# A decoder step on one core: side work held to its place in the order of emission, and the first two row blocks of w_up taken by turns

## The chip, the cores and the metric

The kernel runs on one core of a Trainium2 chip. The metric is the device time of one execution in microseconds (us), the median of several. Five engines share the work: TensorE (PE, matrix products and transposes), VectorE (DVE), ScalarE (ACT), GpSimd (POOL) and SyncE (SP, which only issues transfers). Each engine takes its own instructions strictly in the order in which they stand on it; an instruction that waits holds up all that stand behind it.

## What is computed

One layer of a hybrid decoder, for a prompt of 2048 tokens and 32 sample tokens (8 sequences of 4), with a model width of 1024, all in float32:

```
h = rms_norm(x, norm_pre_mix)
q, k, v, z1, z2, g_a, g_b = project_inputs(h, w_in, b_gate)
...
    outs.append(o)                       # three groups of dilated windows
    lses.append(lse)
o_a = merge_dilations(outs, lses)        # softmax over the groups' log sums
...
merged = g_a * (o_a @ w_ao) + g_b * (o_b @ w_bo)
x = x + rms_norm(merged @ w_out, norm_post_mix)
h2 = rms_norm(x, norm_pre_ffn)
f = jnp.square(jax.nn.relu(h2 @ w_up)) @ w_down
x = x + rms_norm(f, norm_post_ffn)
```

The branch `o_b` is a chunked gMLP gate. The sample tokens attend to caches of 128, 512 and 2048 old rows beside their own.

## The kernel before

**Products.** Each float32 matrix is split into a high and a low part, and a product is three matmuls (high by high, high by low, low by high). The high part is a cast on ACT, the low part a subtraction on POOL or DVE (L264 and L268 for the weights of the first stages, L1303 and L1304 in the feed-forward part, L311 and L312 for transposed rows). PE is fed from these.

**Stages.** The prompt is taken in two halves (s = 0, with the sample tokens, and s = 1). For each half come the projections and the attention for six pairs of a head pair and a window group (`project`, `attention`), the gMLP gate, the mix and the output rows (`out_rows`, with the norms). Then `ffn` does w_up for half 0, w_down for half 0, and the same for half 1. In the profile: attention of half 0 from 95 to 285 us and, as its tail, on to about 395; gMLP and mix of half 0 to 737, output rows to 880; attention of half 1 to 1190; gMLP and mix to 1515, output rows to 1600; w_up and w_down behind that. The feed-forward products are Strassen's seven products of half-size blocks (`SEVEN`): `up` takes 16 row blocks u of w_up, for each the seven products p in order, and gathers each product into the blocks that use it.

**The main chain in attention.** PE makes the scores (L670), DVE adds the mask and takes the minimum (L672, listed as ISA or CUSTOM_DVE), ACT takes the exponential (L676), PE transposes and multiplies by the values (L718), and ACT or DVE copies the result out (L175, L177).

**Side work.** What has no place of its own in this is written as Python generators in four lanes. Lane 0 has the attention itself, the norms and other steps of the main line. Lane 1 has `merge` (the softmax over the window groups, 16 blocks in each half, fetched from DRAM into `junk`; lines L778 to L795), `moved` (normed rows of the output to the channel layout `h2`, each half) and `differences` (differences of the blocks of `h2`, by `differ`, L1271 to L1274). Lane 2 has `sample_attention` (L880, L881, L917, L926 on DVE and L927, L929 on POOL), `pre_mix_behind` (the norm of the next half's prompt rows: L357, L359, L361 on ACT, L363 on DVE) and the sample's gate. Lane 3 has `weight_sums`, which adds blocks of w_up and w_down in DRAM by accumulating transfers that POOL issues (L1253), for use in Strassen's products. `tick()`, called between the matmuls of the main line, takes one step of lanes 0, 1 and 2; lane 3 is stepped each time that a set number of columns has gone through PE. `drain` takes all steps that a lane still has.

**The order on an engine.** The order in which the Python code emits instructions is not the order in which they stand on an engine. A scheduler lays all instructions on its own simulated timeline and places each where its operands are ready by that timeline; so an instruction that the timeline holds for ready early can move up past instructions that were emitted before it, main or side. `tc.issue_after(ins)` around an emission forbids that: what is emitted inside stands on its engine behind `ins`. It makes no wait, only an order; L1247 uses it in the kernel before.

Of the kernel before, what the change touches and what calls it, by code (L numbers as in the profile page):

```python
# [2 lines left out]

# [1 line left out]

# [7 lines left out]
AF = mybir.ActivationFunctionType  # L13
# [48 lines left out]
DIFFS = ("t1", "v", "t3", "t4")  # L62
FORMS = ("b11", "b21", "b22") + DIFFS
HALF_T = (TMAX // 2, HALF // 2)


def shape_constants():
# [27 lines left out]
def hybrid_step(ctx: ExitStack, tc: tile.TileContext, ins: dict, outs: list):  # L95
    nc = tc.nc
# [89 lines left out]
    def push(lane, gen):  # L186
        lanes[lane].append(gen)
        return gen

    def step(lane):  # L190
        while lanes[lane]:
            try:
                next(lanes[lane][0])
                return True
            except StopIteration:
                lanes[lane].popleft()
        return False

    def tick(some=(0, 1, 2)):
        for lane in some:  # L200
            step(lane)
# [555 lines left out]
    def merge(s, hp):  # L757

        mt = sm.tile([P, D], F32, tag="t", bufs=1, name="junk")

        def fetch(b):
            m3 = mt[:, (b % 2) * 3 * UW : (b % 2 + 1) * 3 * UW].rearrange("p (g c) -> p g c", g=3)
            nc.sync.dma_start(m3, us[s][hp][b * P : (b + 1) * P])
            return m3

        m3_next = fetch(0)
        for _ in range(6):
            yield
        for b4 in range(2):
            o4 = sm.tile([P, 512], F32, tag="o4", bufs=1, name="o4")  # L770
            for j in range(4):
                b = b4 * 4 + j
                m3 = m3_next
                if b < 7:
                    m3_next = fetch(b + 1)
                nm, l = m3[:, :, 128:130], m3[:, :, 130:132]
                lo = sm.tile([P, 2], F32, tag="mg0", name="lo")
                nc.vector.tensor_reduce(lo, nm.rearrange("p g h -> p h g"), AX, ALU.min)  # L778
                e3 = sm.tile([P, 3, 2], F32, tag="mg1", name="e3")
                nc.vector.tensor_tensor(e3, nm, lo.unsqueeze(1).to_broadcast([P, 3, 2]), ALU.subtract)  # L780
                nc.scalar.activation(e3, e3, AF.Exp, scale=-1.0)
                el = sm.tile([P, 3, 2], F32, tag="mg2", name="el")
                nc.vector.tensor_tensor(el, e3, l, ALU.mult)
                den = sm.tile([P, 2], F32, tag="mg3", name="den")
                nc.vector.tensor_reduce(den, el.rearrange("p g h -> p h g"), AX, ALU.add)
                rd = sm.tile([P, 2], F32, tag="mg4", name="rd")
                nc.vector.reciprocal(rd, den)
                nc.vector.tensor_tensor(e3, e3, rd.unsqueeze(1).to_broadcast([P, 3, 2]), ALU.mult)
                U = m3[:, :, :P].rearrange("p g (h d) -> p g h d", h=2)
                nc.vector.tensor_tensor(U, U, e3.unsqueeze(3).to_broadcast([P, 3, 2, 64]), ALU.mult)  # L790
                yield
                o1 = o4[:, j * P : (j + 1) * P]
                nc.gpsimd.tensor_tensor(o1, m3[:, 0, :P], m3[:, 1, :P], ALU.add)
                nc.gpsimd.tensor_tensor(o1, o1, m3[:, 2, :P], ALU.add)
                yield  # L795
            for _ in range(6):
                yield
            pt = ps.tile([P, 512], F32, tag="t", name="pt")
            for j in range(4):
                nc.tensor.transpose(pt[:, j * P : (j + 1) * P], o4[:, j * P : (j + 1) * P], ident)  # L800
            cs = slice(b4 * 512, b4 * 512 + 512)
            split(oa[:, hp, 0, cs], oa[:, hp, 1, cs], pt, nc.vector)
            yield
# [319 lines left out]
    def out_rows(s, behind=None):  # L1123
# [50 lines left out]
        def moved():  # L1174

            for b in range(n_rows):
                y, n = of(b)
                if s == 1:
                    y = sm.tile([P, D], F32, tag="x", name="xt")
                    nc.sync.dma_start(y, n1_d[b * P : (b + 1) * P])  # L1180
                    for _ in range(4):
                        yield
                for _ in range(3):
                    if paces[0] < 4 * (b + 1) + 2:
                        yield
                while paces[0] < 4 * (b + 1):
                    yield
                for _ in to_h2(s, y, n, b * P):
                    yield
                    yield  # L1190
# [65 lines left out]
    def differences(s):  # L1256

        n = HALF_T[s]
        for k in range(4):
            u, l = (sm.tile([P, 2, TMAX // 2], F32, tag="x", name="xt")[:, :, :n] for _ in range(2))  # L1260
            nc.sync.dma_start(u, h2_d[s][k])
            nc.sync.dma_start(l, h2_d[s][k + 4])
            for _ in range(4):
                yield
            for i, out in enumerate(differ(u[:, 0, :], u[:, 1, :], l[:, 0, :], l[:, 1, :], u[:, 0, :], l[:, 1, :], l[:, 0, :])):
                nc.sync.dma_start(hd_d[s][i, k], out)
            yield
# [50 lines left out]
    def ffn():  # L1318
# [56 lines left out]
        def product_bank(s):  # L1375
            if s == 0:
                return po[0].tile([P, 1024], F32, tag="d", name="pd")
            return po[0].tile([P, 512], F32, tag="e", name="pe", bufs=6)
# [25 lines left out]
        def up(s, ops):  # L1404
            n = HALF_T[s]
            at = {X11: 0, X21: 1, X22: 2, X12: 5}
            ws = weight_stream([up_form(a, u) for u in range(16) for a, _, _ in SEVEN])
            for u in range(16):
                o = u % 2 * 7 * n
                blk = [ov[:, o + i * n : o + (i + 1) * n] for i in range(7)]  # L1410
                X = {x: blk[i] for x, i in at.items()}
                for p, (a, b, uses) in enumerate(SEVEN):
                    w = next(ws)
                    x = ops[b]
                    pt = product_bank(s)
                    for k in range(4):
                        mults(s, pt, w[:, :, k], x[k], k == 0, k == 3)
                        if k in (1, 3):
                            tick()
                    gather(result(s, pt), uses, X)  # L1420
                    for q in ((), (), (), (X22,), (X11,), (X21,), (X12,))[p]:
                        nc.scalar.activation(X[q], X[q], AF.Relu, scale=1.0 if q in (X11, X12) else -1.0)
                        nc.scalar.square(X[q], X[q])
                    if p == 5:
                        nc.sync.dma_start(f_d[s][u, :, 0:3], ov[:, o : o + 3 * n].rearrange("p (i c) -> p i c", i=3))
                differ(X[X11], X[X12], X[X21], X[X22], blk[3], blk[4], blk[6])
                nc.sync.dma_start(f_d[s][u, :, 3:7], ov[:, o + 3 * n : o + 7 * n].rearrange("p (i c) -> p i c", i=4))

        def f_form(s, form, g):
            return f_d[s][4 * g : 4 * g + 4, :, FORMS.index(form)].rearrange("u p c -> p u c")  # L1430
# [303 lines left out]
```

## Time and profile before

| | |
|---|---|
| median of 3 runs | 2915.31 us (2912.81 to 2915.8) |
| the profiled execution | 2921.58 us, span of the profile 2919.9 us |
| PE busy | 2846.7 us, 97% of the span |
| DVE, ACT, POOL busy | 1274.9, 1247.7, 1258.7 us, 44, 43 and 43% |
| granted clock of PE, mean | 0.99 |

The span is the time from the first to the last instruction that the profile shows. "Busy" leaves out waiting. The granted clock is the share of full speed at which PE was let run in a stretch: 1.00 is the upper of its two levels (2.4 GHz), 0.50 the lower (1.2 GHz), and what lies between is a mean over a stretch that has both. A releaser, behind "<-", is the instruction or transfer that came last before a waiting instruction could start.

### The profile page before, as it was taken

How to read it: one execution, taken by the hardware profiler on the slowest of the kernel's cores; microseconds unless marked ns; L12 is line 12 of the kernel's file. 1: busy time of each engine (PE TensorE's matmuls, PEld its weight loads, DVE VectorE, ACT ScalarE, POOL GpSimd, SP SyncE). 2: the span in 40 equal slices, each digit the busy share in tenths (PEclk: the TensorE clock that was granted, in tenths of full speed). 3: DMA queues.
4: the chain of work that ended last, by engine and by line, in shares of the span. 5: the costliest groups of instructions: out<-in, count | busy, mean ns of one | idle time of the engine just before them, and what ended most of it. 6: DMA issues, size and time to landing. Idle time of an engine off the chain costs nothing. (4 is left out here: it accounts for less than half of the span.)

```text
span 2919.9 us, 45510 instructions
## 1 busy us (share of the span) xinstructions
PE 2846.7 (97%) x17434; PEld 2586.2 (89%) x17434; DVE 1274.9 (44%) x2208; ACT 1247.7 (43%) x2439; POOL 1258.7 (43%) x1098
## 2 busy tenths in 40 slices
PE   8998999989999999999999999999999999999998
PEld 8997999989888888888888999999999888878887
DVE  4558356452363344430024555443343644452235
ACT  5443452213453444431135544454343654454334
POOL 3346333453213344243341344445555744445553
PEclk9999999999999999999999999999999999999999
DMA  5755545553658444444326877576665765676655
GB/s 165 195 167 159 151 117 154 146 156 94 189 172 235 126 120 124 109 110 106 81 94 220 282 252 254 181 250 207 204 200 189 238 208 183 197 264 203 192 187 173
DMA packets 463691, 515.00 MB, mean 176 GB/s; under 512 B 25457, under 2 KB 359857, under 8 KB 454258
## 3 DMA queue, kind: packets, MB, share of 16 engines
q1 hardware_dynamic: 452384, 475.06, 51.0%
q0 software_dynamic: 10944, 36.97, 7.0%
q8 instruction: 137, 2.24, 0.3%
q14 instruction: 80, 0.66, 0.1%
q10 hardware_dynamic: 146, 0.07, 0.0%
HBM read 396.44 MB, written 182.68 MB: 198 GB/s over the span
## 5 line engine op out<-in xcount | busy, mean ns | idle before, releaser
L284 PE MATMUL pg<-act,wh 128*128 128x352 f32 (+3 forms) x3424 | 945.5, 354 | 2.8 <-DVE xt L1095 2.0
L1304 POOL TENSOR_TENSOR wf<-raw,wf 128x512 fp32r<-128x512 f32 x444 | 627.5, 1415 | 703.1 <-ACT wf L1303 652.9
L284 PEld LDWEIGHTS pg<-act,wh 128*128 128x128 f32 x3424 | 613.8, 191 | 52.5 <-DVE xt L1095 2.3
L284 PE MATMUL pg<-act,wl 128*128 128x352 f32 (+3 forms) x1712 | 604.2, 353 | 3.3 <-POOL wl L268 3.3
L1303 ACT CAST wf<-raw 128x512 fp32r<-128x512 f32 x444 | 274.9, 620 | 496.4 <-PE pd L1393 188.4
L268 POOL TENSOR_TENSOR wl<-raw,wh 128x512 fp32r<-128x512 f32 (+1 forms) x212 | 273.8, 1318 | 345.9 <-ACT wh L264 319.8
L1393 PE MATMUL pd<-act,wf 128*128 128x264 f32 x2880 | 366.7, 287 | 10.7 <-ACT act L1303 4.9
L1393 PEld LDWEIGHTS pd<-act,wf 128*128 128x128 f32 x2880 | 358.5, 191 | 11.9 <-ACT act L1303 5.1
L284 PEld LDWEIGHTS pg<-act,wl 128*128 128x128 f32 x1712 | 325.3, 190 | 30.4 <-POOL wl L268 3.6
L1493 PE MATMUL pe<-wf,act 128*128 128x512 f32 (+1 forms) x984 | 224.3, 389 | 0.3 <-POOL wf L1304 0.2
L1493 PEld LDWEIGHTS pe<-wf,act 128*128 128x128 f32 x984 | 181.6, 188 | 42.1 <-POOL wf L1304 0.6
L264 ACT CAST wh<-raw 128x1024 fp32r<-128x1024 f32 (+1 forms) x105 | 106.5, 1015 | 259.3 <-PE pg L284 202.8
L1402 DVE TENSOR_TENSOR ov<-pd,ov 128x528 f32<-128x528 f32 x140 | 96.3, 704 | 203.5 <-PE pd L1393 202.9
L1393 PE MATMUL pd<-pair,wf 128*128 128x264 f32 x1440 | 183.9, 284 | 0.3 <-POOL wf L1304 0.3
L1393 PE MATMUL pe<-act,wf 128*128 128x512 f32 x768 | 182.6, 392 | 0.1
L1393 PEld LDWEIGHTS pd<-pair,wf 128*128 128x128 f32 x1440 | 178.2, 188 | 0.5 <-POOL wf L1304 0.5
L1393 PEld LDWEIGHTS pe<-act,wf 128*128 128x128 f32 x768 | 143.8, 188 | 32.9 <-issue 0.3
L1304 DVE TENSOR_TENSOR act<-flat,act 128x1024 fp32r<-128x1024 f32 (+1 forms) x76 | 101.8, 1342 | 157.5 <-ACT act L1303 157.2
L1402 DVE TENSOR_TENSOR ov<-pe,ov 128x512 f32<-128x512 f32 x136 | 91.5, 687 | 136.8 <-PE pe L1393 125.9
L676 ACT ACTIVATE ov<-ov 128x256 f32<-128x256 f32 (+1 forms) x192 | 91.7, 478 | 123.9 <-DVE ov L672 121.3
L1393 PE MATMUL pd<-oa,wf 128*128 128x264 f32 x1056 | 135.3, 284 | 0.0
L1393 PEld LDWEIGHTS pd<-oa,wf 128*128 128x128 f32 x1056 | 131.0, 188 | 0.1
(301 smaller groups left out, 4205.3 us busy)
## 6 DMA issues: line engine op xcount, KB each, us to landing
raw<-in_w_in_dram SPq DMA_DIRECT2D x84, 512.0 KB, 4.4
raw<-up_sums SPq DMA_DIRECT2D x128, 256.0 KB, 4.4
raw<-down_sums SPq DMA_DIRECT2D x128, 256.0 KB, 3.9
flat<-f SPq DMA_DIRECT2D x48, 528.0 KB, 4.4
raw<-in_w_up_dram SPq DMA_DIRECT2D x96, 256.0 KB, 3.2
raw<-in_w_down_dram SPq DMA_DIRECT2D x96, 256.0 KB, 3.9
flat<-f SPq DMA_DIRECT2D x48, 512.0 KB, 3.8
f<-ov SPq DMA_DIRECT2D x16, 1056.0 KB
```

The lines of the kernel that those rows point to most:

```text
L264: nc.scalar.copy(wh[:, :o], raw[:, :o])
L268: eng.tensor_tensor(wl[:, c], raw[:, c], wh[:, c].bitcast(F32), ALU.subtract)
L284: nc.tensor.matmul(pt[:, :n], a[:, o : o + P], b, start=(i == 0 and j == 0), stop=(i == last and j == 2))
L676: nc.scalar.activation(pb[:, h, :w], pb[:, h, :w], AF.Exp, scale=-1.0, bias=stats[:, u, h : h + 1], accum_out=stats[:, u, 2 + h : 3 + h],)
L1303: nc.scalar.copy(high, raw)
L1304: eng.tensor_tensor(low, raw, high.bitcast(F32), ALU.subtract)
L1393: nc.tensor.matmul(pt[:, o : o + n], w[:, a], x[:, b, c : c + n], start=first and j == 0, stop=last and j == 2)
L1402: nc.vector.tensor_tensor(X[to], res, X[add], ALU.add)
L1493: nc.tensor.matmul(pts[i][:, cs], x[k][:, c, t * P : (t + 1) * P], w[:, d, 0, cs], start=k == 0 and j == 0, stop=k == 15 and j == 2,)
```

## The change

Each step of lanes 1 and 2 is now wrapped so that what it emits stands, on PE, DVE, ACT and POOL, behind the last instruction that was emitted on that engine before the step. For lane 3 the same holds on POOL alone. Lane 0 stays free. In `merge` a block has one more empty step (three in place of two), and in `moved` (half 1) and `differences` eight steps in place of four lie between the fetch of a block and its use. In `up` for half 0 the first 14 products, those of row blocks 0 and 1, are taken by turns: product p of block 0, product p of block 1, then the next p; the stream of weights follows the same order. The number of matmuls and of transfers is the same.

```diff
+ENGINES = (
+    mybir.EngineType.PE, mybir.EngineType.DVE, mybir.EngineType.Activation, mybir.EngineType.Pool
+)
+ORDERED = ((), ENGINES, ENGINES, ENGINES[3:])
...
+    @contextmanager
+    def in_order(*engines):
+
+        left = set(engines)
+        with ExitStack() as held:
+            for ins in reversed(list(nc.cur_bb.bb.instructions)):
+                if not left:
+                    break
+                if ins.engine in left:
+                    left.discard(ins.engine)
+                    held.enter_context(tc.issue_after(ins))
+            yield
+
     def step(lane):
         while lanes[lane]:
             try:
-                next(lanes[lane][0])
+                with in_order(*ORDERED[lane]):
+                    next(lanes[lane][0])
                 return True
...
                 nc.gpsimd.tensor_tensor(o1, o1, m3[:, 2, :P], ALU.add)
+                yield
                 yield
...
-                    for _ in range(4):
+                    for _ in range(8):
                         yield
...
-            for _ in range(4):
+            for _ in range(8):
                 yield
             for i, out in enumerate(differ(u[:, 0, :], u[:, 1, :], l[:, 0, :], l[:, 1, :], u[:, 0, :], l[:, 1, :], l[:, 0, :])):
...
-            ws = weight_stream([up_form(a, u) for u in range(16) for a, _, _ in SEVEN])
...
+            order = [(u, p) for u in range(16) for p in range(7)]
+            if s == 0:
+
+                order[:14] = [(u, p) for p in range(7) for u in range(2)]
+            ws = weight_stream([up_form(SEVEN[p][0], u) for u, p in order])
+            for u, p in order:
+                _, b, uses = SEVEN[p]
+                blk = blks[u % 2]
```

**DVE in the attention of half 0.** The first piece is the kernel before, a stretch of the scheduled order on DVE in which a merge block (L788, L790), the sample attention (L917, L926) and the mask-add of the main chain (ISA, L672) meet:

```order
L926 TENSOR_TENSOR ov<-ov,xt 128x512
L790 TENSOR_TENSOR junk<-junk,e_2369 128x3x128
L788 TENSOR_TENSOR e_2455<-e_2455,rd 128x6
L917 TENSOR_TENSOR xt<-ov,xt 128x512
L790 TENSOR_TENSOR junk<-junk,e_2455 128x3x128
L917 TENSOR_TENSOR ov<-ov,xt 128x512
L672 ISA ov<-ps,con 128x256
L672 ISA ov 128x1
```

The second piece is the changed kernel near the same place; L937 and L946 are the lines L917 and L926 of before, L691 is L672:

```order
L564 COPY smp<-pg 128x32
L691 ISA ov<-ps,con 128x256
L691 ISA ov 128x1
L946 TENSOR_TENSOR ov<-ov,xt 128x512
L691 ISA ov<-ps,con 128x256
L691 ISA ov 128x1
L937 TENSOR_TENSOR xt<-ov,xt 128x512
L946 TENSOR_TENSOR ov<-ov,xt 128x512
L937 TENSOR_TENSOR xt<-ov,xt 128x512
L691 ISA ov<-ps,con 128x256
L691 ISA ov 128x1
```

Before, six instructions of the side work stand between one mask-add and the next here; in the changed kernel one, then three, and the merge's stand elsewhere.

**ACT in the output rows of half 0.** The names ss_7470 and ss_7484 tell two norms apart: ss_7470 is of a row block of the main line (`ov`), ss_7484 of the next half's prompt rows (`xt`, lane 2), whose load is one of the transfers. Before:

```order
L357 ACTIVATE junk,ss_7470<-ov 128x512 x2
L359 ACTIVATE half<-ss_7470,eps_t 128x1
L357 ACTIVATE junk,ss_7484<-xt 128x512
L361 ACTIVATE sd<-ss_7470,half 128x1
L357 ACTIVATE junk,ss_7484<-xt 128x512
L359 ACTIVATE half<-ss_7484,eps_t 128x1
```

In the changed kernel (L376, L378 and L380 are L357, L359 and L361 of before):

```order
L376 ACTIVATE junk,ss_7470<-ov 128x512 x2
L378 ACTIVATE half<-ss_7470,eps_t 128x1
L380 ACTIVATE sd<-ss_7470,half 128x1
L376 ACTIVATE junk,ss_7484<-xt 128x512 x2
L378 ACTIVATE half<-ss_7484,eps_t 128x1
```

The first square sum of the prompt rows moved from ahead of the last step of the main row's norm to behind it.

**PE at the start of w_up.** The operands are `act`, `oa` and the pairs; each row is a run of matmuls, 24 to a product. Before:

```order
L1393 MATMUL pd<-act,wf 128x264 x48
L1393 MATMUL pd<-oa,wf 128x264 x2
L1393 MATMUL pd<-pair_14310,wf 128x264 x12
L1393 MATMUL pd<-pair_14311,wf 128x264 x2
L1393 MATMUL pd<-oa,wf 128x264 x22
L1393 MATMUL pd<-pair_14311,wf 128x264 x10
L1393 MATMUL pd<-act,wf 128x264 x48
```

In the changed kernel (L1413 is L1393):

```order
L1413 MATMUL pd<-act,wf 128x264 x96
L1413 MATMUL pd<-oa,wf 128x264 x48
L1413 MATMUL pd<-pair_14310,wf 128x264 x12
L1413 MATMUL pd<-pair_14311,wf 128x264 x12
L1413 MATMUL pd<-pair_14310,wf 128x264 x12
L1413 MATMUL pd<-pair_14311,wf 128x264 x12
L1413 MATMUL pd<-act,wf 128x264 x22
```

Four products stood ahead of the fifth operand (the second run on `act`) before, and eight stand there now.

## Rows read from the trace of the kernel before

**Rows 1.** The page: busy time, share of the span and instructions of each engine
```profile
PE 2846.7 (97%) x17434; PEld 2586.2 (89%) x17434; DVE 1274.9 (44%) x2208; ACT 1247.7 (43%) x2439; POOL 1258.7 (43%) x1098
```

**Rows 2.** Windows by stage: width, busy us of each engine, PE clock, DMA share, GB/s
```profile
95.00:285.00 190.00, 170.44 (x1120) 164.32 (x1119) 129.88 (x307) 79.26 (x227) 100.28 (x108) 0.96 0.62 171
585.00:640.00 55.00, 48.05 (x273) 46.02 (x274) 41.84 (x42) 8.29 (x15) 36.42 (x27) 0.94 0.63 173
737.00:880.00 143.00, 137.10 (x886) 122.49 (x886) 73.74 (x117) 72.80 (x205) 25.20 (x26) 0.96 0.57 172
880.00:1190.00 310.00, 304.68 (x1745) 263.23 (x1744) 120.94 (x354) 133.19 (x364) 121.18 (x166) 0.99 0.56 149
1290.00:1515.00 225.00, 225.00 (x997) 184.29 (x996) 33.09 (x48) 51.57 (x69) 78.38 (x66) 1.00 0.33 88
1600.00:1640.00 40.00, 34.14 (x250) 33.21 (x249) 27.33 (x32) 25.34 (x46) 14.23 (x11) 0.91 0.86 294
1640.00:1790.00 150.00, 145.15 (x1182) 144.61 (x1182) 79.02 (x101) 65.89 (x108) 63.29 (x48) 0.99 0.84 272
```

**Rows 3.** Windows of L1393 alone, at full clock and behind a wait
```profile
1602.80:1608.90 6.10, 6.10 (x50) 6.10 (x51) 1.00 1.01 339
1619.70:1628.40 8.70, 8.68 (x49) 8.68 (x50) 0.66 0.69 238
```

**Rows 4.** Waits of PE: line waited for: us in total, times, longest
```profile
PE ps L670 <- DVE ov L672: 23.2, 14, 3.4
...
PE pd L1393 <- ACT act L1303: 4.9, 1, 4.9
PE pd L1393 <- DVE ov L1402: 4.8, 3, 2.5
...
PE pg L284 <- POOL wl L268: 3.3, 1, 3.3
```

**Rows 5.** Timeline of DVE in the first attention: start us, duration us
```profile
250.09 0.68 DVE L917 TENSOR_TENSOR xt<-ov,xt 128x512 f32<-128x512 f32 x1
250.69 0.81 DVE L790 TENSOR_TENSOR junk<-junk,e 128x384 f32<-128x384 f32 x1
251.43 1.78 DVE L917 TENSOR_TENSOR ov<-ov,xt 128x512 f32<-128x512 f32 x1
253.13 0.41 DVE L672 CUSTOM_DVE_ANT_0 ov<-ps,con 128x256 f32<-128x256 f32 x1
```

**Rows 6.** DVE by line and form, 130 to 275 us: count, busy us, mean ns
```profile
L917 DVE TENSOR_TENSOR xt<-ov,xt 128x512 f32<-128x512 f32 x10 | 11.5, 1146 | 2.1 <-DMA ov<-in_cache_kv_w_dram 2.0
L881 DVE TENSOR_REDUCE xt<-ov 128x8 f32<-128x512 f32 x16 | 10.6, 677 | 0.0
```

**Rows 7.** Timeline of POOL near 628 us
```profile
628.25 0.81 POOL L1253 DMA_DIRECT2D up_sums<-up_sums  x1 [6.78 <-DMA up_sums<-in_w_up_dram]
```

**Rows 8.** Timeline of all engines, 782 to 785 us
```profile
782.35 0.63 ACT L357 ACTIVATE junk<-xt 128x512 f32<-128x512 f32 x1 [8.74 <-DMA xt<-in_x_prompt_dram]
...
783.29 0.16 DVE L363 RECIPROCAL rs<-sd 128x1 f32<-128x1 f32 x1 [10.45 <-ACT sd L361]
...
784.30 1.12 PE L327 MATMUL ps<-con,ov 128*128 128x128 f32 x4 [5.90 <-DVE ov L1168]
```

**Rows 9.** Waits of DVE: line waited for: us in total, times, longest
```profile
DVE lo L778 <- DMA junk<-us: 46.0, 18, 9.2
...
DVE xt L1271 <- DMA xt<-h: 24.5, 6, 7.0
...
DVE el L783 <- ACT e L781: 0.4, 2, 0.2
```

**Rows 10.** Timeline of ACT, the fill of the fifth product's operand
```profile
1618.60 1.07 ACT L1303 CAST act<-flat 128x1056 fp32r<-128x1056 f32 x1 [0.28 <-DMA flat<-h]
```

**Rows 11.** A row of the waits of ACT
```profile
ACT ov L175 <- PE pu L718: 60.3, 33, 5.1
```

**Rows 12.** Windows of L917 alone, the first attention
```profile
95.00:285.00 190.00, 30.65 (x30) 0.96 0.62 171
```

More of the change, by code (lines that the diff above doesn't have):

```diff
@@ L1 @@
 from collections import deque
-from contextlib import ExitStack
+from contextlib import ExitStack, contextmanager
 import numpy as np
@@ L1406, in up @@
             at = {X11: 0, X21: 1, X22: 2, X12: 5}
-            ws = weight_stream([up_form(a, u) for u in range(16) for a, _, _ in SEVEN])
-            for u in range(16):
-                o = u % 2 * 7 * n
[L1410 to L1427, printed above, removed]
@@ new lines, in up @@
+            blks = [[ov[:, o + i * n : o + (i + 1) * n] for i in range(7)] for o in (0, 7 * n)]
+            order = [(u, p) for u in range(16) for p in range(7)]
[5 more added lines that the diff above has]
+                blk = blks[u % 2]
+                X = {x: blk[i] for x, i in at.items()}
+                w = next(ws)
+                x = ops[b]
+                pt = product_bank(s)
+                for k in range(4):
+                    mults(s, pt, w[:, :, k], x[k], k == 0, k == 3)
+                    if k in (1, 3):
+                        tick()
+                gather(result(s, pt), uses, X)
+                for q in ((), (), (), (X22,), (X11,), (X21,), (X12,))[p]:
+                    nc.scalar.activation(X[q], X[q], AF.Relu, scale=1.0 if q in (X11, X12) else -1.0)
+                    nc.scalar.square(X[q], X[q])
+                o = u % 2 * 7 * n
+                if p == 5:
+                    nc.sync.dma_start(f_d[s][u, :, 0:3], ov[:, o : o + 3 * n].rearrange("p (i c) -> p i c", i=3))
+                if p == 6:
+                    differ(X[X11], X[X12], X[X21], X[X22], blk[3], blk[4], blk[6])
+                    nc.sync.dma_start(
+                        f_d[s][u, :, 3:7], ov[:, o + 3 * n : o + 7 * n].rearrange("p (i c) -> p i c", i=4)
+                    )
```

## The prediction

> **What bounds the kernel now.** I began with the busy times of the page: TensorE (PE) is busy 2846.7 of 2919.9 us [rows 1], so a change that takes no matmul away can win at most the 73 us in which PE stands idle, and what a lowered clock costs beside them. Next I cut the span by stage and read, for each, PE's busy time and the granted clock [rows 2]. The reader is to see that the loss lies in a few stages. A stage's loss is its width less PE's busy time, plus its width times one minus the granted clock: attention of half 0 (95 to 285 us) 19.6 + 0.04 x 190 = 27.2; the stretch from 585 to 640 us 6.95 + 0.06 x 55 = 10.2; the output rows of half 0 (737 to 880) 5.9 + 0.04 x 143 = 11.6; attention of half 1 (880 to 1190) 5.3 + 0.01 x 310 = 8.4; the start of w_up (1600 to 1640) 5.9 + 0.09 x 40 = 9.5; behind it (1640 to 1790) 4.85 + 0.01 x 150 = 6.4. Together 73 us, and from 1290 to 1515 us, as an example of the rest, PE is busy throughout. The clock is part of it because PE comes out of a longer wait at half speed: the same 48 or so matmuls of L1393 took 6.1 us at a granted 1.00 and 8.7 us at 0.66 behind a wait of 4.9 us [rows 3], so that wait cost 2.6 us more than its length.
>
> Then I asked whom PE waits for [rows 4]. The mask-add L672 on VectorE (DVE) leads, with 23.2 us in 14 waits; the next ones are single waits of 3.3 to 5.9 us [rows 4, 8]. So the question for every edit is what stands ahead of L672 on DVE, of L361 on ScalarE (ACT), of L268 on GpSimd (POOL) and of L1303 on ACT.
>
> **The change part by part.** It adds no arithmetic. Lanes 1 and 2 may no longer be placed ahead of the last instruction emitted before them on PE, DVE, ACT and POOL; lane 3 likewise on POOL. That forbids being earlier, never being later. Three waits in emission get longer, and 14 products of w_up change places.
>
> *Attention of half 0.* Before the mask-add at 253.13 us DVE did three lane instructions in a row, 0.68 + 0.81 + 1.78 us [rows 5], while PE waited for L672. In the order of the first fence on DVE this is one of seven such strings between 230 and 270 us, at the means of [rows 6] some 25 us long; behind the change I count four there, some 10 us. I take half of the stage's 27.2 us as won, 13.6. The ends: 5 if most strings only go to other mask-adds, since L917 still has to be done in this stage, 20 if the waits for L672 fall with the strings.
>
> *The stretch 585 to 640.* On POOL an accumulating DMA L1253 of lane 3 waited 6.8 us for the transfer before it and stood ahead of L268 [rows 7], for whose low weights PE waited 3.3 us [rows 4]. Its half clock is about half of 0.06 x 55, 1.7. With lane 3 held, the accumulation stands behind that L268. Against the 5.0 us I set 2 for a longer string of sample instructions now ahead of L1093: -3 net, between 0 and -5.
>
> *The output rows of half 0.* ACT's L357 on the next half's prompt rows waited 8.74 us for its load, and stood ahead of L361 of a main row; DVE's L363 waited 10.45 us for that, and PE 5.90 us [rows 8]. In the fence on ACT, L361 now stands ahead of that L357. The gap of 5.9 goes, with half of the stage's 5.7 us of clock, 2.9; the load is still late, so the next norm is late in its turn, for which I leave 1.5: -7, between -3 and -8.8.
>
> *Attention of half 1.* DVE waited 24.5 us in 6 waits in L1271 for h2 rows [rows 9]; mask-adds are queued behind. Eight steps in place of four between load and use leave that much more time for the load. I take -5 of 8.4, between 0 and -8.4: the merge's wait for its own rows (L778, 46.0 us in 18) is not cured by that.
>
> *w_up by turns.* PE waited 4.9 us for the ACT fill L1303 of the fifth product's operand [rows 4], which ACT ended at 1618.60 + 1.07 = 1619.7 us [rows 10]. 50 matmuls take 6.1 us [rows 3] and a product has 24, so behind eight products in place of four the operand is wanted at 1602.8 + 192 x 0.122 = 1626.2 us: 6.5 us to spare. Gain 4.9 + 2.6 = -7.5, at least -4.9. Behind it (1640 to 1790) PE waited 4.8 us in three waits for L1402 [rows 4], where the differences' L1273 and L1274 stood ahead; half of 6.4, -3, between 0 and -6.4.
>
> *What is new.* The merges of half 1 end later: where the merge's steps are driven out, 12 are left in place of 4, and PE's transposes for them stand ahead of the projection that needs them. That lies in the stretch in which PE never waits [rows 2], so a wait there is all loss. No row shows it; from nothing to the longest wait for a merge row, 9.2 us [rows 9], with some 3 us of half clock. I take +6, nearer the upper end because a burst has no cover. The extra yield itself costs nothing, as it emits nothing.
>
> Sum: -13.6 - 3 - 7 - 5 - 7.5 - 3 + 6 = -33 us. The profiled execution took 2921.6 us with a span of 2919.9, 6.3 us above the median of the runs; taken off the median of 2915.3 that gives 2882 us.
>
> One rule speaks against this. The two-input lane instruction L917 takes 1.15 us on average and 1.78 at its longest here, the one-input L881 of the same size 0.68 [rows 5, 6]. The Trainium skill, page "SBUF — State Buffer", section "Who interferes with whom", says that a VectorE instruction with two SBUF inputs contends with a GpSimd instruction that reads SBUF, that one then blocks the other for its length, and that the order of issue decides which. The trace agrees in that only the two-input kind is stretched. Where the new order leaves the share of L917 that falls beside POOL's reads as it is, the sum stays at -33; by the rule, where that share grows, it is that of the third rival below, about -17.
>
> **The rivals.** (1) *Slower: the merge stalls DVE.* A merge block's L783 needs the exponential of ACT, which must now stay behind the last main instruction there; and L783 follows L780 with little between. Before, this wait was 0.4 us in all [rows 9]. If every one of the 32 merge blocks held DVE for the mean of ACT's wait in L175, 60.3 / 33 = 1.83 us [rows 11], that is 59 us, and the kernel ends at 2882 + 59 = 2941 us. It decides from 33 / 32 = 1.0 us a block. Against it: most merge blocks lie in stages where DVE has time to spare.
> (2) *The transfers bind the start of w_up.* The DMA engines are busy 0.86 and 0.84 of 1600 to 1640 and of 1640 to 1790 us [rows 2], 160 of 190; without 10.5 us of stalls that is 0.89. If weights then come late, 7.5 + 3 are not won: 2893 us. With a tail of the merges at its upper end of 12 in place of 6, 2899.
> (3) *The lane instructions are stretched.* If each of the 30 L917 of the first attention [rows 12] took 1.78 in place of 1.15 us, because they fall beside POOL's work more often, that is 19 us of DVE in the stage where PE waits for it: the 13.6 are gone, 2896 to 2901 us. By the rule of the Trainium skill named above another order may do this, in either direction.
> (4) *Little changes.* The scheduler fills the same gaps with other instructions, each wait is replaced by one as long: 2910 to 2920 us. For it speaks that several waits (the sample's L917 ahead of L1093 and L1095, ACT's L175 ahead of w_up) keep their order.
>
> **How the numbers follow.** My forecast gets 0.58 (its own range 2864 to 2900), rival 1 0.12, rival 2 0.11, rival 3 0.06, rival 4 0.10, and 0.03 is left for what I don't see. A difference of 0.2%, 5.8 us, is about what a measurement of this kernel can tell from no change. Faster are the forecast, rivals 2 and 3 and a little of the rest: 0.77; same is rival 4 with a small part of rival 1, where the stall eats just the gain: 0.11; slower is most of rival 1 and of the unseen: 0.12. The low end takes all bounds at their best, 20 + 5 + 8.8 + 8.4 + 7.5 + 6.4 = 56 us, less a tail of at least 3: 2862. The high end takes rivals 2 and 3 whole and half of rival 4: 2913.
>
> **What would show it.** Right: PE's waits for L672 at 10 to 15 us in place of 23; no wait of PE for L327's input near 784 us and no 8.74 us of ACT ahead of L361; no POOL L1253 in the middle of the low weights; no PE wait at the fifth product's operand, and clock 1.00 there; granted clock 0.98 or more in the first attention. Wrong: DVE idle ahead of L783 for more than 10 us in all; PE idle between 1290 and 1515 us beyond 10 us; L1303 on ACT waiting for weights behind 1610 us; or a first attention as long as before.

## The result, and the profile after

The changed kernel took 2875.01 us (median of 4 runs, 2871.7 to 2876.15), the kernel before beside it 2914.06 us (4 runs, 2912.65 to 2915.8): a ratio of 0.9864, with a 95% interval from 0.9847 to 0.9881, so 39 us faster. Run again on another chip it gave 0.9854 (0.9837 to 0.9871). 2882 us were forecast, in a range from 2862 to 2913.

The first rows of the page of the changed kernel answer to [rows 1]:

```profile
span 2873.2 us, 45422 instructions
...
PE 2827.3 (98%) x17434; PEld 2573.0 (90%) x17434; DVE 1283.5 (45%) x2208; ACT 1254.3 (44%) x2443; POOL 1259.4 (44%) x1098
```

PE's busy time fell by 19 us with the same 17434 matmuls. At most 15 us of it is time at half clock: the mean granted clock rose from 0.990 to 0.995, which is 29.2 us of 2919.9 before and 14.4 us of 2873.2 now. The windows by stage follow, cut where the same number of matmuls is done as at the bounds of [rows 2] (columns as there):

```profile
95.30:273.00 177.70, 165.62 (x1119) 159.10 (x1119) 127.55 (x297) 79.48 (x226) 91.24 (x101) 0.99 0.57 167
...
384.30:568.50 184.20, 184.20 (x1166) 182.70 (x1165) 118.62 (x212) 63.75 (x101) 79.95 (x74) 1.00 0.54 148
568.50:624.50 56.00, 46.99 (x275) 44.66 (x274) 38.88 (x43) 8.10 (x15) 36.83 (x28) 0.91 0.58 162
721.50:860.50 139.00, 136.56 (x887) 121.74 (x886) 74.14 (x117) 74.68 (x205) 25.73 (x26) 0.98 0.60 181
860.50:1160.00 299.50, 299.50 (x1744) 260.24 (x1743) 121.69 (x353) 132.87 (x363) 120.47 (x165) 1.00 0.57 154
1160.00:1255.80 95.80, 94.36 (x481) 79.30 (x481) 48.32 (x108) 48.20 (x64) 39.55 (x38) 1.00 0.42 110
1255.80:1480.80 225.00, 225.00 (x997) 184.14 (x997) 34.38 (x53) 55.80 (x73) 83.37 (x73) 1.00 0.45 112
1566.70:1598.70 32.00, 31.00 (x250) 30.36 (x249) 24.51 (x27) 22.68 (x42) 16.22 (x11) 1.00 0.92 310
1598.70:1741.30 142.60, 142.60 (x1181) 142.60 (x1181) 69.29 (x93) 69.47 (x112) 61.33 (x48) 1.00 0.76 246
```

The first attention (177.7 in place of 190 us), the attention of half 1 (299.5 for 310) and both stretches of w_up (32.0 for 40, 142.6 for 150) are shorter. PE is all but full in them, the first attention apart (165.6 of 177.7 us). The stretch that was 585 to 640 us is as long as before, 56, though its old waits are gone. This is how the spans of the two profiled executions differ, stage by stage, beside what was forecast; the last column is the profile of the later run of the same kernel, for how far two executions lie apart:

| stage of the kernel before, us | forecast | changed | run again |
|---|---|---|---|
| 95 to 285, attention of half 0 | -13.6 | -12.3 | -13.0 |
| 285 to 395, its tail | 0 | +1.3 | +1.3 |
| 395 to 585, gMLP and mix of half 0 | 0 | -5.8 | -5.8 |
| 585 to 640, mix | -3 | +1.0 | +0.8 |
| 737 to 880, output rows of half 0 | -7 | -4.1 | -4.2 |
| 880 to 1190, attention of half 1 | -5 | -10.3 | -10.3 |
| 1190 to 1290, gMLP of half 1 | 0 | -4.3 | -4.3 |
| 1290 to 1515, mix of half 1 | +6 | +0.1 | +0.1 |
| 1600 to 1640, start of w_up | -7.5 | -7.9 | -7.9 |
| 1640 to 1790, w_up | -3 | -7.3 | -7.3 |

The stages left out moved by 2 us or less each. The profiled spans differ by 46.7 us and the medians by 39, because the profiled execution of before was 7 us above its median; a stage that an edit doesn't touch moved by up to 1.7 us between profiles (seen in the run with the turns alone, below).

The waits of PE in the changed kernel, to be set against [rows 4]:

```profile
PE ps L689 <- DVE ov L691: 9.3, 10, 1.7
PE ps L955 <- DVE xt L1113: 8.2, 1, 8.2
...
PE pg L303 <- ACT flat L549: 2.3, 1, 2.3
...
PE pu L737 <- DVE rd L806: 1.3, 1, 1.3
PE pd L1413 <- ACT ov L180: 1.0, 1, 1.0
PE pg L317 <- POOL wl L287: 1.0, 1, 1.0
```

The mask-add (now L691) went from 23.2 us in 14 waits to 9.3 in 10, and the waits for L1168, for the fifth product's operand and for the low weights near 630 us are no longer there. One wait of 8.2 us is new. These are its rows on DVE:

```profile
602.44 1.63 DVE L946 TENSOR_TENSOR prod<-prod,junk 128x512 f32<-128x512 f32 x1
607.04 0.69 DVE L937 TENSOR_TENSOR prod<-gbc,zs 128x512 f32<-128x512 f32 x1 [2.97 <-DMA gbc<-smp]
607.64 0.51 DVE L1113 TENSOR_TENSOR xt<-xt,ps 128x352 f32<-128x352 f32 x1
```

The chain reads from below: L1113 frees the bank of partial sums that PE's L955 needs. L1113 stands behind a string of sample instructions (L937, L946), the last of which waited 2.97 us for its rows. From 576.3 to 607.6 us DVE did nothing but such instructions, 24 of them. Behind the wait PE ran at half clock, up to 615 us (a window, columns as above):

```profile
608.20:615.00 6.80, 6.01 (x18) 4.21 (x19) 2.13 (x5) 0.00 (x0) 5.22 (x5) 0.50 0.41 135
```

So the string cost PE 8.2 us of waiting and some 3.4 us (6.8 x 0.50) of clock.

### The profile page after: what moved, and what is told of

It is laid out like the page before. It is cut to its first block, busy times and chain, and to the rows that moved or that the text cites. A ratio compares the mean times of both kernels' runs of the same rounds, so it can differ in the third digit from the quotient of the medians.

```text
span 2873.2 us, 45422 instructions
## 1 busy us (share of the span) xinstructions
PE 2827.3 (98%) x17434; PEld 2573.0 (90%) x17434; DVE 1283.5 (45%) x2208; ACT 1254.3 (44%) x2443; POOL 1259.4 (44%) x1098
## 4 chain that ended last, share of the span: by engine, by line
PE 88%; DMA 5%; DVE 5%; issue 1%; ACT 1%; POOL 1%; SPq 0%; DVEq 0%; POOLq 0%; ACTq 0%
PE pg L303 31%; PE pd L1413 21%; PE pe L1413 11%; PE pe L1521 10%; PE pg L317 6%; PE pu L737 2%; PE ps L303 1%; PE pt L723 1%; PE pt L346 1%; PE ps L689 1%; PE ps L690 1%; DMA xt<-h 1%; PE pt L1048 0%; DMA ov<-in_cache_kv_w_dram 0%; DMA xt<-in_cache_kv_w_dram 0%
## 5 line engine op out<-in xcount | busy, mean ns | idle before, releaser
L287 POOL TENSOR_TENSOR wl<-raw,wh 128x512 fp32r<-128x512 f32 (+1 forms) x212 | 274.6, 1319 | 405.2 <-ACT wh L283 360.2
L1413 PE MATMUL pd<-act,wf 128*128 128x264 f32 x2880 | 361.4, 285 | 1.9 <-ACT ov L180 1.0
L1413 PEld LDWEIGHTS pd<-act,wf 128*128 128x128 f32 x2880 | 354.1, 189 | 2.5 <-ACT ov L180 1.4
L1413 PE MATMUL pd<-pair,wf 128*128 128x264 f32 x1440 | 183.2, 284 | 0.0
L1413 PE MATMUL pe<-act,wf 128*128 128x512 f32 x768 | 182.6, 392 | 0.1
L1413 PEld LDWEIGHTS pd<-pair,wf 128*128 128x128 f32 x1440 | 177.9, 188 | 0.0
L1413 PEld LDWEIGHTS pe<-act,wf 128*128 128x128 f32 x768 | 143.8, 188 | 32.9 <-issue 0.3
L1413 PE MATMUL pd<-oa,wf 128*128 128x264 f32 x1056 | 135.0, 284 | 0.0
L1413 PEld LDWEIGHTS pd<-oa,wf 128*128 128x128 f32 x1056 | 130.8, 188 | 0.0
```

Of the source, the lines that this page charges most:

```text
L287: eng.tensor_tensor(wl[:, c], raw[:, c], wh[:, c].bitcast(F32), ALU.subtract)
L1413: nc.tensor.matmul(pt[:, o : o + n], w[:, a], x[:, b, c : c + n], start=first and j == 0, stop=last and j == 2)
```

## The experiments

**The parts by themselves.** Four kernels with one part each. The first is the changed kernel with the old order of products:

```diff
             order = [(u, p) for u in range(16) for p in range(7)]
-            if s == 0:
-
-                order[:14] = [(u, p) for p in range(7) for u in range(2)]
```

> The changed kernel with w_up of half 0 in its old order of products; the rest of the change stays. Theory (the order of the side work brings what is won ahead of 1600 us, the turns what is won behind it): the gain of 39 us falls by the 8 us of the stage 1600 to 1640, and the wait of 4.9 us for the fifth product's operand comes back: 27 to 31 us faster than before. Rival (the turns also bring what is won from 1640 to 1790, 7.3 us): 21 to 26 us faster. Other rival (the operand now comes earlier, since the steps ahead of it are done earlier, and the turns bring nothing): 36 us or more faster.

Measured: 2879.4 us, ratio 0.9875 (0.9862 to 0.9889), 36 us. That is what the third theory expected, but the trace contradicts that theory: the wait is back, and 1600 to 1640 us is as long as before (39.7 us).

```profile
1585.98 4.25 PE L1413 MATMUL pd<-act,wf 128*128 128x264 f32 x21 [5.47 <-ACT act L1323]
```

The stage from 1640 to 1790 us stays 7.3 us shorter without the turns, so the turns bring one stage alone. My expectation came too low in part because it started from a gain of 39 us, where the two measurements of this kernel gave 39 and 43.

The second is the kernel before with that edit alone.

> The kernel before with the turns alone. Theory: all stages ahead of 1600 us as before, the wait for the fifth product's operand gone, 5 to 9 us faster (ratio 0.997 to 0.998). Rival (turns also bring 1640 to 1790): 12 to 16 us faster. Other rival (nothing without the order of the side work): within 3 us.

Measured: 2909.2 us, 0.9975 (0.9965 to 0.9985), 7.3 us faster; 1600 to 1640 took 31.9 in place of 39.8 us, and the later stretch 150.5 as before. The theory holds, and it is one term of the sum measured alone: 7.5 forecast.

The third is the order of the lanes alone, without the longer waits and the turns:

```diff
+                with in_order(*ORDERED[lane]):
+                    next(lanes[lane][0])
```

> The kernel before with the order of lanes 1, 2 and 3 alone: no longer waits, no turns. Theory (the order alone brings the attention of half 0, the output rows and the attention of half 1): 22 to 30 us faster, waits for the mask-add near 10 us. Rival (in the attention of half 1 the gain of 10 us comes from eight steps in place of four): 10 to 20 us faster, and waits of DVE for h2 rows of 4 to 5 us in that stage as before.

Measured: 2891.52 us, 0.9916 (0.9902 to 0.9929), 24.5 us faster, as the theory expected, with 13.3 us of waits for the mask-add, not 10. The attention of half 1 is 9.0 us shorter without the longer waits, so the rival falls there. The fourth is the longer waits alone:

```diff
                 nc.gpsimd.tensor_tensor(o1, o1, m3[:, 2, :P], ALU.add)
+                yield
                 yield
...
-                    for _ in range(4):
+                    for _ in range(8):
                         yield
```

> The kernel before with the longer waits in emission alone (three empty steps in a merge block, eight steps for h2 rows). Theory (the scheduler undoes them, since it may move the steps up again): within 5 us of before. Rival (the slack is what helps the attention of half 1): 8 to 14 us faster, and that stage some 10 us shorter.

Measured: 2917.84 us, 0.9999 (0.9988 to 1.001). Alone they bring nothing. The stretch 1640 to 1790 is 7.3 us shorter here too, and the next is 6.0 longer: the collision of the differences with w_up only moved. The rows on DVE of that kernel (L1272 to L1275 are L1271 to L1274 of before):

```profile
1789.04 0.69 DVE L1273 TENSOR_TENSOR xt<-xt 128x512 f32<-128x512 f32 x1 [3.62 <-DMA xt<-h]
1789.64 1.80 DVE L1272 TENSOR_TENSOR ov<-ov 128x528 f32<-128x528 f32 x1
...
1796.57 2.92 DVE L1403 TENSOR_TENSOR ov<-pd,ov 128x528 f32<-128x528 f32 x4
```

The differences wait 3.6 us for h2 rows and take 7.5 us, and the gather of the products (L1403) stands behind them. With the order held, this wait is not there.

So the turns bring 7, the order alone 24.5, the waits alone 0, and order and waits together 36: **12 us come only from both** (the 24.5 and the 36 are each good to about 4 us). This is the costliest place in the kernel with the order alone, on DVE and then on ACT:

```profile
386.68 0.16 DVE L797 TENSOR_REDUCE lo<-junk 128x2 f32<-128x6 f32 x1 [7.29 <-DMA junk<-us]
386.88 0.17 DVE L799 TENSOR_TENSOR e<-junk,lo 128x6 f32<-128x6 f32 x1
```

```profile
387.08 0.21 ACT L800 ACTIVATE e<-e 128x6 f32<-128x6 f32 x1 [7.25 <-DVE e L799]
387.63 0.21 ACT L800 ACTIVATE e<-e 128x6 f32<-128x6 f32 x1 [0.34 <-DVE e L799]
387.85 1.28 ACT L1008 ACT_TABLE_LOAD   x1
389.15 1.09 ACT L1008 ACTIVATE ov<-pt 128x512 f32<-128x512 f32 x2
```

A merge held to its place waited 7.29 us for its rows; ACT's exponential L800 waited for it with the gMLP's L1008 behind it, and PE waited 3.96 us for that. The two stages that meet here, up to 585 us, are 7.8 us longer than in the kernel with order and waits.

**Which of the longer waits.** The order, and the one more empty step in a merge block:

> The kernel before with the order of the lanes and the one more empty step in a merge block; no longer wait for h2 rows, no turns. With the order alone it was 25 us faster, with all three longer waits 37. Theory (most of the 12 us between them is the merge: held to its place, it waits on DVE and ACT for its rows, and the empty step puts that much more between fetch and use): 32 to 37 us faster, no wait of PE near 390 us for ACT's L1008 behind a merge's exponential. Rival (the h2 rows make the difference): 24 to 29 us faster.

Measured: 2881.22 us, 0.9880 (0.9864 to 0.9896), 35 us. The theory holds: the empty step in the merge brings nearly all of the 12, and PE's wait near 390 us is gone. What the eight steps for h2 rows add once the order holds is 1.4 us by the ratios, less than these can tell from nothing.

**Which of the lanes.** The changed kernel with one lane set free at a time; for lane 1

```diff
-ORDERED = ((), ENGINES, ENGINES, ENGINES[3:])
+ORDERED = ((), (), ENGINES, ENGINES[3:])
```

and likewise for lanes 2 and 3.

> The changed kernel with lane 1 (merges, h2 movements, differences) free again; lanes 2 and 3 held, longer waits and turns as changed. Theory (lane 1 brings what is won in the attention of half 1, 10 us, in the gMLP of half 1, 4 us, and from 1640 to 1790, 7 us): 16 to 24 us faster than before in place of 39, and these three stages as before. Rival (lane 2 alone brings nearly all; the lane 1 steps only stood near): 32 us or more faster.

Measured: 2895.99 us, 0.9929 (0.9915 to 0.9943), 21 us faster. The theory holds for half 1 (attention +5.3 against before, gMLP -0.8), not for 1640 to 1790, which stays at -7.3 while the stretch behind it loses 3.8. The half-1 loss is one wait of 6.3 us for the mask-add:

```profile
913.98 0.71 DVE L1292 TENSOR_TENSOR xt<-xt 128x528 f32<-128x528 f32 x1 [7.62 <-DMA xt<-h]
...
916.09 0.42 DVE L691 CUSTOM_DVE_ANT_0 ov<-ps,con 128x256 f32<-128x256 f32 x1
```

DVE stood 7.62 us in L1292 (L1272 of before) for h2 rows, ahead of two mask-adds. With the lane free, eight steps of slack did not help. That the scheduler had moved the step up is the likely reason; the time at which it was emitted is not shown.

> The changed kernel with lane 2 (sample attention, the norm of the next half's prompt rows, the sample's gate) free again. Theory (lane 2 brings the 12 us of the attention of half 0 and the 4 us of the output rows, and costs the wait of 8.2 us near 608 us with its 5 us of half clock): the two gains go and the cost goes too, 24 to 34 us faster than before. Rival (the attention of half 0 is won by holding the merge): that stage stays 10 us or more shorter, and the kernel ends 40 us or more faster.

Measured: 2878.22 us, 0.9868 (0.9849 to 0.9886), 38 us: within the error of the changed kernel and above the 24 to 34 us of the theory, so that lane 2, held throughout, brings nothing net. In the stages both halves of the theory's mechanism are there, at other sizes. The first attention is only 2.1 us shorter than before, so lane 2 brings 10 of its 12 us; the stretch 585 to 640 is 4.9 shorter than before, so holding lane 2 costs 6 there, and wins 5 just ahead of it (395 to 585 is 0.8 shorter with the lane free, 5.8 with it held; with lane 1 or lane 3 free these 5.8 us go too, so they hang on all three). The output rows, however, stay 5.1 us shorter with lane 2 free, with ACT in the order of before, a square sum of the prompt rows (`xt`) ahead of L380, which is L361 of before:

```profile
766.98 0.63 ACT L376 ACTIVATE junk<-xt 128x512 f32<-128x512 f32 x1 [0.78 <-DMA xt<-in_x_prompt_dram]
...
767.61 0.28 ACT L380 ACTIVATE sd<-ss,half 128x1 f32<-128x1 f32 x1
```

The prompt rows came 0.78 us late in place of 8.74 [rows 8], so the old order cost nothing. What ended the wait shows in the next kernel.

> The changed kernel with lane 3 (weight sums on POOL) free again. Theory (an accumulating transfer that waits on POOL ahead of the low weights costs PE one or two waits like that of 3.3 us near 630 us): 31 to 37 us faster than before, with PE waits for L287 of 2 to 6 us. Rival (lane 3 is placed well once lanes 1 and 2 are held): 38 us or more faster, no difference to the changed kernel.

Measured: 2885.46 us, 0.9895 (0.9880 to 0.9910), 31 us: 9 to 12 us of the gain hang on lane 3, more than I had put on it, but not where I expected. No PE wait for L287 beyond 0.3 us came back. The first attention is 7.7 us shorter in place of 12.3, with a wait of PE of 4.2 us at 140 us, behind this on DVE:

```profile
137.45 0.69 DVE L900 TENSOR_TENSOR ov<-xt,ov 128x512 f32<-128x512 f32 x1 [5.78 <-DMA ov<-in_cache_kv_w_dram]
```

A sample instruction waits 5.78 us for cache rows. The transfers of 118 to 142 us by queue, in this kernel and then in the changed one (packets, MB, share of the 16 engines):

```profile
q1 hardware_dynamic: 6187, 4.26, 60.3%
q0 software_dynamic: 144, 1.05, 26.5%
```

```profile
q1 hardware_dynamic: 7125, 4.91, 69.3%
```

With lane 3 free, as before, an accumulating transfer of 1 MB of the weight sums runs here (queue q0) and takes 26% of the DMA engines' time while the cache rows are on their way; with lane 3 held it is not in this stretch.

The wait in the output rows came back too, 3.3 us of the old 5.9, though ACT now has the new order. The waits of PE, then POOL and DVE (L346 is L327 of before, L1188 is L1168):

```profile
PE ps L346 <- DVE ov L1188: 3.3, 1, 3.3
```

```profile
762.49 0.81 POOL L1273 DMA_DIRECT2D down_sums<-down_sums  x1 [6.23 <-DMA down_sums<-in_w_down_dram]
```

```profile
773.69 0.75 DVE L1188 TENSOR_SCALAR ov<-ov,rs 128x1024 f32<-128x1024 f32 x1 [6.73 <-DMA x<-ov]
```

POOL issues an accumulating transfer, and a store that was issued 2.3 us later (`x<-ov`) keeps DVE's L1188 waiting for 6.73 us. In the kernel before the same stands there: L1253 at 769.21 us, the load of the prompt rows issued at 769.99 and in at 782.35. Queue q0 from 765 to 790 us of that kernel:

```profile
q0 software_dynamic: 144, 1.05, 25.0%
```

All four kernels with lane 3 free (before, turns alone, longer waits alone, and this one) have this transfer in the stretch and a wait of PE of 3.1 to 5.9 us; none of the ten profiles with lane 3 held has the wait, whatever the order on ACT. So it is lane 3's order that ended it. The third wait of this kind is one of 3.3 us up to 399 us: DVE waits 4.66 us for a merge's rows while 1.05 MB accumulate, and the stage 395 to 585 us is as long as before (+0.8).

**Which of the engines.** Lanes 1 and 2 held on DVE alone, lane 3 on POOL:

```diff
-ORDERED = ((), ENGINES, ENGINES, ENGINES[3:])
+ORDERED = ((), ENGINES[1:2], ENGINES[1:2], ENGINES[3:])
```

> The changed kernel with lanes 1 and 2 held on DVE alone (lane 3 on POOL as changed). Theory (the mask-adds on DVE are what the lanes stand ahead of; ACT and PE matter only in the output rows): 30 to 38 us faster than before, the attention of both halves as short as in the changed kernel within 3 us. Rival (an order on DVE that ACT and PE don't keep makes new waits between engines): 25 us faster or less.

Measured: 2873.09 us, 0.9852 (0.9836 to 0.9869), against 0.9854 for the changed kernel run beside it: 43 us, above the 30 to 38 of the theory. The order on DVE (and POOL) carries the whole gain; holding PE and ACT too changes nothing in the total that can be measured, though single stages trade up to 4 us (against the changed kernel the tail of the first attention is 4.4 longer and 395 to 585 us 3.3, the first attention itself 2.7 shorter and the gMLP of half 1 2.1).

**The new wait, and a better kernel.** Lane 2 set free in the mix of half 0, where the string of sample instructions stands ahead of L1113:

```diff
-                with in_order(*ORDERED[lane]):
+                with in_order(*(() if lane in loose else ORDERED[lane])):
...
                     push(2, sample_attention(1))
+                    loose.add(2)
...
+        loose.clear()
         if s == 0:
             push(2, sample_branch())
```

> The changed kernel with lane 2 free in the mix of half 0 alone. Theory (the wait of 8.2 us near 608 us comes from some 24 sample instructions that now stand in one piece ahead of L1113 on DVE): it goes with its 5 us of half clock, waits of 1.4 and 2.0 us near 570 us as before come back; 44 to 50 us faster than before, 5 to 10 faster than the changed kernel. Rival (the late transfer that DVE waits 3 us for, or PE's own place, sets it): the wait stays at 5 us or more, and the kernel is within 4 us of the changed one.

Measured: 2870.4 us (2869.56 to 2870.71), 0.9843 (0.9828 to 0.9858), 46 us faster than before. The wait of 8.2 us is gone and the old short ones are back, as the waits of PE show (L1115 and L1117 of this kernel are L1093 and L1095 of before):

```profile
PE ps L690 <- DVE ov L692: 9.8, 10, 2.1
PE pg L304 <- DVE xt L1117: 3.5, 2, 2.0
...
PE ps L304 <- DVE xt L1115: 1.5, 1, 1.5
```

So the place of the string was the cause; the waits for rows inside it (0.3, 0.6 and 3.0 us) can be 3.9 of the 8.2 us at most. The gain on the changed kernel is some 3 to 6 us by the ratios, whose intervals overlap. On top of that, a few empty steps in the sample attention after rows that had to be waited for:

```diff
+                late_rows = i == 0
                 while True:
...
+                    late_rows = True
                     yield None
-                if i == 0:
-                    for _ in range(4):
+                if late_rows:
+                    for _ in range(6):
```

> The kernel with lane 2 free in the mix of half 0, and in the sample attention six empty steps, not none, after a group of sample rows had to be waited for (four before the first rows become six). Theory (DVE's waits of some 5 us for sample rows near 122 and 172 us, which PE feels as 1.3 to 2.2 us each and one half-clock stretch, lie in that slack): 2 to 5 us faster than with lane 2 free alone, 47 to 51 us faster than before. Rival (the later sample steps stand ahead of other mask-adds): no faster than the 45 us of lane 2 free alone.

Measured: 2868.11 us (5 runs, 2865.22 to 2870.91), 0.9832 (0.9816 to 0.9849). The changed kernel on the same chip took 2873.5 us (4 runs, 2871.51 to 2878.01): each run of the one is below each run of the other, though the two intervals of the ratios overlap. It has the lowest median here. Against lane 2 free alone the ratios give 3 us, the size that the theory expected, but their intervals overlap, so the rival is not excluded. The windows of the first attention and of the mix's end:

```profile
94.50:256.70 162.20, 160.68 (x1120) 158.17 (x1119) 105.56 (x274) 77.59 (x217) 74.81 (x92) 1.00 0.52 155
564.80:622.00 57.20, 47.59 (x276) 45.60 (x275) 40.94 (x44) 8.67 (x15) 37.08 (x29) 0.91 0.61 165
```

PE is busy in 160.7 of 162.2 us in the first attention, which is 28 us shorter than before. But the tail behind it is 12 us longer, with two waits for the mask-add of 1.3 and 2.6 us, and a wait of 8.0 us is back in the mix, behind a string of sample instructions again: a lane that is set free may still be placed in one piece. What the slack won in one stage it gave back for the most part in two others.

## Why the forecast was right, and where its terms were not

**The sum.** -33 us were forecast and -39 measured, -43 when run again. That the totals lie so near is in part luck. The stages that did better than their terms make 26 us (gMLP and mix of half 0 5.8, the merges' tail 5.9, attention of half 1 5.3, gMLP of half 1 4.3, 1640 to 1790 us 4.3, the start of w_up 0.4), those that did worse 9.5 (585 to 640 us 4.0, output rows 2.9, attention of half 0 with its tail 2.6). And the profile of before, from which the terms were read, was 7 us above the median. The turns were right in cause and size (-7.5; -7.9 in the profile, -7.3 in runs of their own). The strings ahead of the mask-add were right in size (-13.6; -12.3 and -13.0 in the profiles) and in part in cause.

**Attention of half 0.** I had counted strings of lane instructions. Part of the loss was a transfer of lane 3 that ran beside the cache rows, shown by the two transfer views above; the kernel with lane 3 free keeps 4.6 us of the loss. With lane 2 free 10 us of the gain go, so the two shares overlap.

**585 to 640 us.** Wrong in sign; with the stage ahead, from 395 us, -4.8 against -3. The step that failed is the "2 for a longer string of sample instructions": it cost 8.2 us and 3.4 us of half clock, 11.6. Against it all of the stage's 10.2 us of loss went, the waits for L1095 and L268 with their half clock, and not the 5.0 that I had counted. The string grew from 18 instructions, which took DVE from 596.9 to 618.9 us and cost PE no wait for L1093, to 24 that took 31 us and had to wait for rows; no row of before had a price for that. Nor is it shown that holding lane 3 ended the wait of 3.3 us for L268: with lane 3 free and the others held it stays away too.

**The output rows.** -7 forecast, -4.1 measured. The wait of 5.9 us for L327's input went, but not by the step that I gave. ACT's order of L361 was not what ended it: with lane 2 free, and with the lanes held on DVE alone, ACT has the old order and the wait stays away. The load was late behind an accumulating transfer of lane 3, as the kernel with lane 3 free shows; I had put nothing on that transfer here. At the end of the stage a wait of 2.3 us for L549 with half clock behind it is new (PE's waits above). It comes from DVE, where L1188 of the sample's rows waits for their store ahead of L557, and ACT's L556 and L549 wait for L557:

```profile
847.22 0.74 DVE L1188 TENSOR_SCALAR flat<-flat,rs 32x1024 f32<-32x1024 f32 x1 [6.46 <-DMA x<-flat]
```

With lane 1 free this wait is not there, and the stage is 9.5 us shorter than before.

**Half 1.** The attention won 10.3 us for 5; the gMLP 4.3 for 0. Both come from lane 1: set free, they go. The bound of 8.4 us that I gave for the attention was too low. A granted clock rounded to 0.99 explains little of it: there were two stretches at half clock of 3.4 us each, which cost half their length, 3.4, and with the idle 5.3 that makes 8.7; some 1.5 us remain that I can't name. The reason I gave, eight steps in place of four, is not the one: the order alone wins 9.0 us there, and the slack without the order nothing.

**The tail of the merges in half 1.** +6 forecast, +0.1 measured. PE is busy in all of the 225 us [rows 2 and the window at 1255.80 above]. The merge's rows were in time for the 12 steps: DVE waits for none of them in this stretch, and only 2.1 us for a merge's exponential, beside other work of PE.

**Behind the start of w_up.** -3 forecast from 1640 to 1790 us, -7.3 measured, beyond the bound of 6.4. The order alone brings 5.6 there; the longer waits alone bring 7.3 and lose 6.0 in the next stage.

**The rivals.** The first (the merge stalls DVE) began as described: DVE's wait in L802, which is L783 of before, rose from 0.4 us [rows 9] to

```profile
DVE el L802 <- ACT e L800: 24.5, 18, 5.1
```

and so beyond the 10 us that I had named as a sign against the forecast. PE felt 1.3 us of it in one wait (L806, above); 12 of the 24 us lie in the gMLP of half 1, where DVE has time to spare. The second (transfers at the start of w_up) fell: the DMA engines are 0.92 busy from 1566.7 to 1598.7 us, and PE waits for no weight there. The third (stretched lane instructions) fell:

```profile
95.30:273.00 177.70, 28.07 (x28) 0.99 0.57 167
```

28.07 / 28 = 1.00 us each, 30.65 / 30 = 1.02 before [rows 12] (the 1.15 us from which I priced this rival is the mean of ten of them alone). The rule of the Trainium skill, page "SBUF — State Buffer", section "Who interferes with whom", expects no change either, since the share beside POOL did not grow: 26 of the 30 ran beside a POOL TENSOR_TENSOR before, 21 of the 28 do now. The trace agrees with the rule: of the 148 instructions of L880, L917 and L926 of this size in the kernel before, the 58 without such an instruction beside them took 0.69 us on average and 0.87 at most, the other 90 took 1.17 and up to 1.79. The fourth fell as a whole; from 585 to 640 us it is what happened, 10.2 us of loss replaced by 11.6.

**What stays open.** Which lane's order ended the wait for L268 near 630 us; why the three lanes must all be held for the 5.8 us from 395 to 585 us; and 1.5 us of the attention of half 1.

## What to carry to other kernels

Side work that a scheduler may move up is best held to its place on the one engine where it meets the main chain, here VectorE (and GpSimd for the lane that issues transfers); but a step that is held waits for its own transfer with the main chain behind it, so order and slack belong together: 24.5 and 0 us apart, 36 together. Not every lane is worth holding: with lane 1 or lane 3 set free 19 to 22 and 9 to 12 us were lost, with lane 2 nothing that can be measured. Where a stage has side work enough to fill an engine, its instructions can end up in one long string with a wait at the end, whether the lane is held or free: look for the longest string ahead of each instruction that PE waits for, and spread it. And an engine's order also sets when its transfers run: look at the transfers by queue in the stretch where a load or a store comes late, before an order of instructions is blamed for the wait.

## What the runs showed of the hardware

In 118 to 142 us, with lane 3 free, 1.05 MB of accumulating transfers took 26.5% of the 16 DMA engines' time and 4.26 MB of plain ones 60.3%: 6.1 us of all engines for a MB against 3.4, 1.8 times as long. Packets of one size show that this is not the path or the size: up to 640 us of the kernel before, the 2048 accumulating packets of 8192 bytes between DRAM tensors took 0.70 us on average, the 2048 plain ones of the copies of w_up (L1248) 0.33 us, 2.1 times. Whether the adding makes this or the queue from POOL is not separated here. I had counted weight sums as POOL time alone.

Behind an accumulating transfer of 1 MB other transfers came late: the prompt rows took 12.4 us from issue to use in the kernel before (769.99 to 782.35), and at most 4.4 in the kernel with lane 2 free (762.57 to 766.98), where none ran beside them.
